# A two-block model on one core: router and last expert group in written order, the last group's first half in two column parts, MLP products of 512 and 256 columns

## The chip, the core and the metric

The kernel runs on one core of a Trainium2 chip, as one launch. The metric is device time in microseconds (us), the median of several executions. TensorE (PE) multiplies, VectorE (DVE), ScalarE (ACT) and GpSimd (POOL) work on SBUF and PSUM, and one DMA queue, issued by SyncE (SP), brings the weights from HBM. All dense data is float32. Durations are of one profiled execution.

## The reference

256 tokens of width 1024 go through two blocks of one layer each. The first block ends with a mixture of experts, the second with a gated MLP:

```python
def hier_moe(xn, w_group, b_group, w_er, b_er, w_e_in, w_e_out):
    g_logits = (xt @ w_group) + b_group
    g_sel = jnp.argmax(g_logits, axis=-1)                      # top-1 of 4 groups
    e_logits = ((xt @ w_er) + b_er).reshape(T, N_GROUPS, EXPERTS_PER_GROUP)
    e_in_group = jnp.take_along_axis(e_logits, g_sel[:, None, None], axis=1)[:, 0]
    top_v, top_i = lax.top_k(e_in_group, TOP_K_INNER)          # top-2 of its 8 experts
    gates = g_prob * jax.nn.softmax(top_v, axis=-1)
    ...
    hdn = lax.ragged_dot(xs, w_e_in, group_sizes)              # 1024 -> 2 x 256
    act = jax.nn.silu(gate_h) * up_h
    ys = lax.ragged_dot(act, w_e_out, group_sizes)             # 256 -> 1024
    ys = ys * gates...
    return jnp.zeros_like(xt).at[tok_sorted].add(ys)

# first block:  h = h + merged @ w_out;  h = h + hier_moe(rms_norm(h, norm2_g), ...);  rms_norm(h, norm_f_g)
# second block: h = rmsnorm(x, ln1); z = h @ w_in  (q, k, v of three attentions, three gates)
#               x = x + merged @ w_o
#               u = causal_dwconv(rmsnorm(x, ln2) @ w_up, conv_w, conv_b)   # 1024 -> 2 x 2816, 3 taps
#               a, b = split(u);  x = x + (silu(a) * b) @ w_down;  rmsnorm(x, ln_f)
```

## The kernel before

Tokens are held as two tiles of 128 (`t` = 0, 1). **Dense products** are made of three products each, to keep float32 precision: weights and activations are split into a high and a low part (`wh`, `wl`; `xx[:, 0]`, `xx[:, 1]`), and high by high, high by low and low by high are added in PSUM. `split` makes the two parts of a weight unit of 1024 columns: ACT copies the high part (L158), VectorE subtracts to get the low part (L159). Three buffers `w0` to `w2` hold split units. `mat_a` (L183 to L185) has the activations as the stationary operand and 512 columns of weights moving; `mat_b` (L190 to L192) has the weights stationary and the 256 tokens moving.

**Weights** come through `Ring`, a list of all loads in the order of their use on one SP queue (L81). A load is issued as soon as it is the next of the list and a slot of its size is free; `done(i)` gives a slot back. Dense units are 512 KB (tile `a`), expert units 1 MB (two of the `a` slots, or slots `r`, `rw`, `rc`). `rw` are the three buffers `w0` to `w2`, lent to the ring while the experts run.

**The router** (L678 to L790): the last dense product of the first block is added to `h` (L694, 512 columns at a time), `h` is transposed (L678), multiplied by the router's weights (L686, tile `prt`), scaled by the rms, and a chain of small VectorE operations picks group and experts of each token (`lgt` L718 to `cm` L730). A product with a triangular matrix gives each token its rank (L734), and from the ranks VectorE makes a selection matrix `sT` of 128 slots (L787, L788), one for each token tile. The gather multiplies `h` by `sT` (L796), `xg` is its result.

**The experts** run in eight groups of four, 32 slots for each. A group takes four pairs of units for the products in (L950), the gated unit, and two pairs of units for the products out (L962), one for each half (512 columns) of the output. The half's rows are multiplied by the gates and split (`yh` L853, `yl` L854), and the scatter (L861) adds them back to token order in `acc`, in PSUM, where `h` stands already. In the list of loads, two dense units of the second block stand ahead of the last two expert units. After the last group `acc` is copied to `h` (L913, L915), `h` is transposed (L922) and split (`uu`, L925, L926), and the second block's first dense product starts on it (`psa`, four units). The V product (L183 to L185 on `uu`) follows, then the rms statistics and their row (`prb`, L1093).

**The MLP** runs over 11 blocks `j` of 2 x 256 columns. `up(j)` is four units of eight 128-column blocks, `mat_b` each, into two PSUM banks; `gated(j)` scales (L1331), does the convolution (L1335 to L1337), silu and product, and splits the result (`ah`, `al`); `down(j)` multiplies by two units of `w_down` (L1362 to L1365, 512 columns). The order on TensorE is `up(j)`, `down(j - 1)`, `up(j + 1)`.

Inside `tc.manual_schedule(engines=...)` the listed engines keep the written order; elsewhere a scheduler orders instructions. PSUM has eight banks, four under the tag `mm` and four under `sm`.

Of the kernel before, what the change touches and what calls it, by code (L numbers as in the profile page):

```python
# [20 lines left out]
P = 128  # L21
# [80 lines left out]
def _build(ctx, tc, nc, a, out):  # L102
# [193 lines left out]
    def keep_warm(n):  # L296

        junk = sm([P, P], name="junk")
        for _ in range(n):
            nc.tensor.matmul(junk, warm, warm, start=True, stop=True)  # L300
# [374 lines left out]
    def h_turned(c, t):  # L675
        pt = sm([P, 4, P])
        for j in range(4):
            nc.tensor.transpose(pt[:, j, :], h[:, t, (4 * c + j) * P:(4 * c + j + 1) * P], ident)  # L678
        hT = m2.tile([P, 4, P], F32, name="hT", tag="hT", bufs=2)
        nc.vector.tensor_copy(hT[:, 0:2, :], pt[:, 0:2, :])  # L680
        nc.scalar.activation(hT[:, 2:4, :], pt[:, 2:4, :], AF.Copy)
        return hT

    def router(c, t, hT):
        for j in range(4):
            nc.tensor.matmul(prt[:, t, :], hT[:, j, :], wr[:, 4 * c + j, :], start=(c == 0 and t == 0 and j == 0),  # L686
                             stop=(c == 1 and j == 3), skip_group_check=True)
# [29 lines left out]
    def route(t):  # L717
        nc.vector.scalar_tensor_tensor(lgt[:, t, 0:36], prt[:, t, :], r2[:, t:t + 1], row("br"), op0=OP.mult, op1=OP.add)  # L718
        nc.vector.max(out=gm[:, t, :], in_=lgt[:, t, 32:40])
        nc.vector.max_index(out=gi[:, t, :], in_max=gm[:, t, :], in_values=lgt[:, t, 32:40])  # L720

        nc.vector.tensor_tensor(ohg[:, t], iota[:, 0:4], gi[:, t, 0:1].to_broadcast([P, 4]), op=OP.not_equal)
        nc.vector.scalar_tensor_tensor(em[:, t], ohg[:, t, :, None].to_broadcast([P, 4, 8]), -BIG,
                                       lgt[:, t, 0:32].rearrange("p (g e) -> p g e", e=8), op0=OP.mult, op1=OP.add)
# [13 lines left out]
    with tc.manual_schedule(engines={mybir.EngineType.PE}):  # L738
# [3 lines left out]
        for t in range(NT):  # L742
            add_to_h(0, t)
# [6 lines left out]
        for t in range(NT):  # L750
            for u in (2, 3):
                mat_a(mTh, mTl, pss, ww[u - 2], [(kk, t) for kk in range(2)], 2 * u, KD, 0, 512, 512)
                if (t, u) == (0, 2):
                    for t2 in range(NT):
                        router(0, t2, hTs[t2])
# [783 lines left out]
```

## Time and profile before

| | |
|---|---|
| median of 3 runs | 883.31 us (882.45 to 883.67) |
| profiled execution | 884.57 us, of which 882.84 are the span from first to last instruction |
| TensorE | busy 834.0 us (94%), mean granted clock 0.988 |
| VectorE | busy 528.7 us (60%) |
| ACT | busy 396.6 us (45%) |
| DMA | 217.79 MB, mean 247 GB/s |

Busy time of TensorE is a time in which at least one product was in flight; it says nothing of how fast the columns went through. Shares are means over stages that differ, so the rows further down are read by stage.

### The profile page before, as it was taken

To read this page: it belongs to the slowest core of one execution; us is meant where nothing else is said; L and a number is where in the kernel's file an instruction comes from. 1 tells how busy PE (TensorE), PEld (TensorE's weight loads), DVE (VectorE), ACT (ScalarE), POOL (GpSimd) and SP (SyncE) were. 2 spreads that over 40 slices of the span, in tenths; PEclk is the share of its full clock that TensorE was granted. 3 is DMA by queue.
4 is the path that set the end of the run, shared out by engine and by line. 5 is a ranking of instruction groups with operands and counts; after the bars stand their busy time and mean duration, and the time that the engine had idled before them with its cause. 6 is when DMAs were issued, how large, how long until landed. Compare 5 with 4: busy or idle time off the path is not lost.

```text
span 882.8 us, 13378 instructions
## 1 busy us (share of the span) xinstructions
PE 834.0 (94%) x5143; PEld 652.4 (74%) x5143; DVE 528.7 (60%) x1055; ACT 396.6 (45%) x621; POOL 34.4 (4%) x44
## 2 busy tenths in 40 slices
PE   7999999999999999778886999999999999999996
PEld 6878789988887544254331888778887999999995
DVE  7887866574565322123112867664496787767876
ACT  6444665554343011101111664575545556555554
POOL 3000101000000000000000100000030000000001
PEclk9999999999999999979999999999999999999999
DMA  8654536879968899999999573336555465555511
GB/s 329 271 167 165 179 130 235 316 248 326 331 267 322 336 422 422 419 418 420 420 421 407 180 234 127 107 120 198 195 166 190 162 192 190 180 188 182 176 62 48
DMA packets 48559, 217.79 MB, mean 247 GB/s; under 512 B 5616, under 2 KB 7296, under 8 KB 36200
## 3 DMA queue, kind: packets, MB, share of 16 engines
q1 hardware_dynamic: 47608, 215.00, 65.6%
q0 software_dynamic: 592, 1.84, 0.7%
q8 instruction: 42, 0.69, 0.3%
q14 instruction: 29, 0.24, 0.1%
q10 hardware_dynamic: 288, 0.03, 0.0%
HBM read 215.77 MB, written 1.07 MB: 246 GB/s over the span
## 4 chain that ended last, share of the span: by engine, by line
PE 49%; issue 26%; DMA 18%; DVE 3%; ACT 2%; POOL 1%; POOLq 0%; SPq 0%; DVEq 0%
PE mm L183 10%; PE mm L185 10%; PE mm L184 10%; DMA r<-in_u_exp 6%; DMA rw<-in_u_exp 5%; DMA a<-in_u_exp 5%; PE sm L950 2%; PE mm L191 2%; PE mm L190 2%; PE mm L192 2%; DVE ww L159 1%; PE sm L796 1%; ACT ww L158 1%; PE sm L1129 1%; PE po L1159 1%
## 5 line engine op out<-in xcount | busy, mean ns | idle before, releaser
L159 DVE TENSOR_TENSOR ww<-a,ww 128x1024 fp32r<-128x1024 f32 (+2 forms) x212 | 256.7, 1212 | 125.1 <-ACT ww L158 116.2
L158 ACT ACTIVATE ww<-a 128x1024 fp32r<-128x1024 f32 (+2 forms) x212 | 220.5, 1042 | 225.9 <-PE mm L185 115.7
L190 PE MATMUL sm<-zz,ww 128*128 128x256 f32 x352 | 99.8, 284 | 0.0
L191 PE MATMUL sm<-zz,ww 128*128 128x256 f32 x352 | 99.7, 283 | 0.0
L192 PE MATMUL sm<-zz,ww 128*128 128x256 f32 x352 | 99.6, 283 | 0.0
L184 PE MATMUL mm<-ww,xx 128*128 128x512 f32 x208 | 82.1, 395 | 3.5 <-DVE ww L159 3.5
L183 PE MATMUL mm<-ww,xx 128*128 128x512 f32 x208 | 82.4, 399 | 0.5 <-ACT ww L158 0.5
L185 PE MATMUL mm<-ww,xx 128*128 128x512 f32 x208 | 81.8, 393 | 0.0
L191 PEld LDWEIGHTS sm<-zz,ww 128*128 128x128 f32 x352 | 67.5, 192 | 0.4
L190 PEld LDWEIGHTS sm<-zz,ww 128*128 128x128 f32 x352 | 67.4, 192 | 0.4
L192 PEld LDWEIGHTS sm<-zz,ww 128*128 128x128 f32 x352 | 67.5, 192 | 0.0
L183 PE MATMUL mm<-ww,uu 128*128 128x512 f32 (+1 forms) x128 | 49.7, 388 | 0.0
L185 PE MATMUL mm<-ww,uu 128*128 128x512 f32 (+1 forms) x128 | 48.8, 381 | 0.0
L184 PE MATMUL mm<-ww,uu 128*128 128x512 f32 (+1 forms) x128 | 48.7, 380 | 0.0
L184 PEld LDWEIGHTS mm<-ww,xx 128*128 128x128 f32 x208 | 39.1, 188 | 12.3 <-DVE ww L159 4.7
L183 PEld LDWEIGHTS mm<-ww,xx 128*128 128x128 f32 x208 | 39.1, 188 | 8.5 <-ACT ww L158 0.7
L185 PEld LDWEIGHTS mm<-ww,xx 128*128 128x128 f32 x208 | 39.1, 188 | 7.9 <-issue 0.3
L950 PE MATMUL sm<-r,xg 128*32 128x512 f32 x304 | 42.4, 613 | 2.5 <-DMA r<-in_u_exp 2.5
L796 PEld LDWEIGHTS sm<-sT,h 128*128 128x128 f32 x256 | 31.9, 205 | 14.1 <-issue 12.9
L796 PE MATMUL sm<-sT,h 128*128 128x128 f32 x256 | 33.7, 293 | 7.3 <-DVE sT L788 7.2
L853 ACT ACTIVATE yh<-sm,sc 128x512 fp32r<-128x512 f32 x16 | 11.0, 687 | 56.9 <-PE sm L962 44.2
L841 ACT ACTIVATE G<-sm 128x256 fp32r<-128x256 f32 x8 | 3.1, 384 | 73.8 <-PE sm L837 73.8
(398 smaller groups left out, 1607.7 us busy)
## 6 DMA issues: line engine op xcount, KB each, us to landing
r<-in_u_exp SPq DMA_DIRECT2D x63, 1024.0 KB, 15.2
a<-in_u_mlp SPq DMA_DIRECT2D x66, 512.0 KB, 4.2
a<-in_u_in SPq DMA_DIRECT2D x59, 512.0 KB, 4.6
a<-in_u_exp SPq DMA_DIRECT2D x20, 1024.0 KB, 19.8
a<-in_u_c SPq DMA_DIRECT2D x40, 512.0 KB, 4.2
rw<-in_u_exp SPq DMA_DIRECT2D x9, 1024.0 KB, 20.0
a<-in_u_wa SPq DMA_DIRECT2D x8, 512.0 KB, 4.5
a<-in_u_wb SPq DMA_DIRECT2D x8, 512.0 KB, 5.8
```

The source lines that it names most:

```text
L158: nc.scalar.activation(wh[:, c:c + step], wt[:, c:c + step], AF.Copy)
L159: nc.vector.tensor_tensor(wl[:, c:c + step], wt[:, c:c + step], wh[:, c:c + step].bitcast(F32), op=OP.subtract)
L183: nc.tensor.matmul(pss[t], lh, rh, start=(k == 0), stop=False)
L184: nc.tensor.matmul(pss[t], lh, rl, start=False, stop=False)
L185: nc.tensor.matmul(pss[t], ll, rh, start=False, stop=(k == kt - 1))
L190: nc.tensor.matmul(ps, wh[:, c:c + P], xx[:, 0, k, :], start=(k == 0 and first), stop=False, skip_group_check=True)
L191: nc.tensor.matmul(ps, wh[:, c:c + P], xx[:, 1, k, :], start=False, stop=False, skip_group_check=True)
L192: nc.tensor.matmul(ps, wl[:, c:c + P], xx[:, 0, k, :], start=False, stop=(k == kt - 1), skip_group_check=True)
L796: nc.tensor.matmul(px[:, k2, :], h[:, t, (k + k2) * P:(k + k2 + 1) * P], sT[:, t, :], start=(t == 0), stop=(t == 1))
L853: nc.scalar.activation(yh, py, AF.Copy, scale=gs)
L950: nc.tensor.matmul(ph[32 * j:32 * j + 32, :], xg[:, k, 32 * j:32 * j + 32], us[j // 2][0][:, (2 * (j % 2) + kk) * 512:(2 * (j % 2) + kk + ...
L1129: nc.tensor.matmul(pl, qv[:, qt * P:(qt + 1) * P], kv[:, :nk], start=True, stop=extra is None)
```

## The change

It has three parts, which don't depend on each other.

**A. The router in written order.** TensorE, and from the last products of the second half on also VectorE and ACT, keep the written order. Both units' products of the first token tile come first, then those of the second tile; the first tile is added to `h`, transposed and put through its first selection steps meanwhile. The second tile's addition to `h` comes in two halves of 256 columns. The 13 steps of the two selection chains are dealt out in turn (`steps`), and the gather is split by token tile (`gather_part`). The three `w` buffers go to the ring one by one, each after its last use (`give`), instead of together.

**B. The last group.** Group 7 gets 24, 24, 24 and 18 small bf16 products on a junk bank behind its four pairs of products in, and 10 more at its end (`keep_warm`). The products out of the first half are made in two parts of 256 columns, and evacuated, scattered and summed by parts. Transposes and the first dense unit of the second block come before the products of the last half. Splits are made by 512 columns at fixed places, and the statistics' squares move ahead of units 2 and 3.

**C. The MLP's up-products.** For the first nine of eleven `j`, `wh` is multiplied by the high and low parts of `zz` together in one product of 512 columns, and `wl` by the high part in one of 256. The two halves of a bank must then be added: ACT copies one out of PSUM, VectorE adds the other (L1510), and `gated` works on the sum in SBUF. Four banks are used instead of two.

The core of the diff:

```diff
-    def add_to_h(c, t):
-        hv = h[:, t, c * 512:(c + 1) * 512]
-        nc.vector.tensor_tensor(hv, pss[t], hv, op=OP.add)
-        junk = sm([P, 512], name="junk")
-        nc.scalar.activation(junk, hv, AF.Square, accum_out=ss2[:, t, c:c + 1])
+    def add_to_h(c, t, c0=0, n=512):
+        hv = h[:, t, c * 512 + c0:c * 512 + c0 + n]
+        nc.vector.tensor_tensor(hv, pss[t][:, c0:c0 + n], hv, op=OP.add)
...
+        def give(x):
+            ring.add_slots(big.tile([P, 2, UNIT], F32, name="rw", tag=f"w{old_w[x]}", bufs=1), 1, 2, moe1 - 10)
+        give(0)
+        mat_a(mTh, mTl, pss, ww[0], [(kk, 0) for kk in range(2)], 4, KD, 0, 512, 512)
+        for t in range(NT):
+            router(0, t)
+        mat_a(mTh, mTl, pss, ww[1], [(kk, 0) for kk in range(2)], 6, KD, 0, 512, 512)
+    with tc.manual_schedule(engines={mybir.EngineType.PE, mybir.EngineType.DVE, mybir.EngineType.Activation}):
+        add_to_h(1, 0)
+        squares(1, 0)
+        mat_a(mTh, mTl, pss, ww[0], [(kk, 1) for kk in range(2)], 4, KD, 0, 512, 512)
+        give(1)
...
+        nc.vector.tensor_copy(hT[0], pt)
+        rms_of(1, 0)
+        mat_a(mTh, mTl, pss, ww[1], [(kk, 1) for kk in range(2)], 6, KD, 0, 512, 512)
         ring_blk(12, 2, moe1 - 14)
...
+        give(2)
+        r0, r1 = route(0), route(1)
+        for i in range(2):
+            add_to_h(1, 1, 256 * i, 256)
+        router(1, 0)
...
+        router(1, 1)
+        steps(r0, 2)
+        rms_of(1, 1)
+        steps(r0, 2)
...
+        for _ in range(5):
+            steps(r1, 1)
+            steps(r0, 1)
+        ranked(0, 0, oneb, code, first=True)
+        ranked(0, 0, upper, cm[:, 0, :], last=True)
...
+        for i in range(2):
+            gather_part(px[i], sT, 2 * i, 2, 0)
+        steps(r1, 4)
...
+            gather_part(px[i], sT, 2 * i, 2, 1)
+            gathered(px[i], xg, 2 * i, 2)
...
-    def products_in(q):
+    def products_in(q, junk):
...
+            if junk is not None:
+                keep_warm((24, 24, 24, 18)[u], junk)
...
+        for i, (w, _) in enumerate(us):
+            for c in range(2):
+                for kk in range(2):
+                    for j in (2 * i, 2 * i + 1):
+                        o = (2 * (j % 2) + kk) * 512 + 256 * c
+                        nc.tensor.matmul(py[c][32 * j:32 * j + 32, :], at[:, kk, 32 * j:32 * j + 32], w[:, o:o + 256],
...
+        rows_part(py[0], 0, 256)
+        scatter_part(0, 0, 256)
+        wh0(0)
+        sums_part(0, 0, 256)
+        rows_part(py[1], 256, 256)
+        wh0(512)
+        pts = turn_k((0, 1), sm)
...
+        unit_by_parts(psa, uu, 0, w0, 0)
+        pts = turn_k((2, 3), sm)
...
+        unit_by_parts(psa, uu, 0, w0, 1)
...
+        py = mm([P, 512])
+        for kk in range(2):
+            for j in range(4):
...
+        rows_part(py, 0, 512)
+        unit_by_parts(psa, uu, 1, w1, 0)
...
+        scatter_part(1, 0, 512)
...
+        unit_by_parts(psa, uu, 1, w1, 1, (0, 1))
...
+        pts = turn_k((4, 5, 6, 7), mm)
+        unit_by_parts(psa, uu, 1, w1, 1, (2, 3))
...
     def up(j):
-        pu = [sm([P, 2, S]) for _ in range(2)]
+        wide = j < NJ - 2
+        pu = [sm([P, 2, S]) for _ in range(4 if wide else 2)]
...
+                    if wide:
+                        nc.tensor.matmul(pu[b], wh[:, c:c + P], zz[:, :, k, :], start=(k == 0), stop=False, skip_group_check=True)
+                        nc.tensor.matmul(pu[b][:, 0, :], wl[:, c:c + P], zz[:, 0, k, :], start=False, stop=(k == KD - 1), skip_group_check=True)
+                    else:
+                        mat_b(pu[b // 2][:, b % 2, :], zz, wh, wl, c, k, KD, b % 2 == 0)
+        if not wide:
+            return pu
+        xs = [e1.tile([P, 2, S], F32, name=f"cx{i}", tag=f"cx{i}", bufs=2) for i in range(2)]
+        for b in range(4):
+            xv = xs[b // 2][:, b % 2, :]
+            nc.scalar.activation(xv, pu[b][:, 1, :], AF.Copy)
+            nc.vector.tensor_tensor(xv, pu[b][:, 0, :], xv, op=OP.add)
+        return xs
```

Where instructions stand. On TensorE, from the last dense products to the first expert products of group 0, before (L678 turns `h`, L686 the router's product, L734 the ranks, L796 the gather, L950 the expert product):

```order
L184 MATMUL mm<-ww,mT 128x512
L185 MATMUL mm<-ww,mT 128x512
L678 MATMUL sm<-ident,h 128x128 x8
L686 MATMUL prt<-wr,hT 128x36 x8
...
L734 MATMUL prk<-cm,upper 128x32
L782 LDWEIGHTS oneb
L782 MATMUL prk<-cm,oneb 128x32
L796 MATMUL sm<-sT,h 128x128 x8
L950 MATMUL sm<-r,xg 32x512 x8
```

and of the change (L684 turns, L688 the router's product, L750 the ranks, L758 the gather in parts, L995 the expert product):

```order
L684 MATMUL sm<-ident,h 128x128 x4
L183 MATMUL mm<-ww,mT 128x512
...
L688 MATMUL prt<-wr,xg 128x36 x4
L684 MATMUL sm<-ident,h 128x128 x2
L684 MATMUL mm<-ident,h 128x128 x2
L688 MATMUL prt<-wr,xg 128x36 x4
L754 MATMUL acc<-h,ident 128x512
...
L758 MATMUL px<-sT,h 128x128 x8
L995 MATMUL sm<-r,xg 32x512 x8
```

The first tile's transposes now stand ahead of the last dense products, and its router product ahead of the second tile's transposes. The eight gather products (four for each token tile) are one row in both; of the change the four of the first tile stand first.

On TensorE at the end of group 7, before (L962 the products out, L861 the scatter, L922 turns `h`, L190 to L192 the dense units of the second block):

```order
L861 MATMUL acc<-yh,G 128x512
L861 MATMUL acc<-yl,G 128x512
L861 MATMUL acc<-yh,G 128x512
L861 MATMUL acc<-yl,G 128x512
L962 MATMUL sm<-r,at 32x512 x8
L922 MATMUL sm<-ident,h 128x128 x8
L190 MATMUL mm<-uu,ww 128x256
```

and of the change (L1134 the products out of the first half, L1180 those of the last half, L1104 the scatter, L1090 turns `h`, L1081 the dense units):

```order
L1134 MATMUL sm<-r,at 32x256 x8
L1104 MATMUL acc<-yh,G 128x256 x2
L1104 MATMUL acc<-yl,G 128x256 x2
L1090 MATMUL sm<-ident,h 128x128 x4
L1104 MATMUL acc<-yh,G 128x256 x2
L1104 MATMUL acc<-yl,G 128x256 x2
L1081 MATMUL psa<-uu,ww 128x256 x12
L1090 MATMUL sm<-ident,h 128x128 x4
L1081 MATMUL psa<-uu,ww 128x256 x12
L1180 MATMUL mm<-r,at 32x512 x8
L1081 MATMUL psa<-uu,ww 128x256 x12
L1104 MATMUL acc<-yh,G 128x512 x2
```

Eight transposes and a whole dense unit (24 products) have moved ahead of the products out of the last half.

On VectorE in one period of the MLP, before (L1331 scales, L1336 and L1337 are the convolution, L159 splits, L1340 multiplies by silu, L233 makes `al`):

```order
L1331 TENSOR_TENSOR cx_10019<-sm,rb_8220 128x512
L1331 TENSOR_TENSOR cx_10020<-sm,rb_8220 128x512
L159 TENSOR_TENSOR ww<-a,ww 128x1024
L1336 SCALAR_TENSOR_TENSOR cy_10017<-cx_10019,cwb,cy_10017 128x255 x2
...
L159 TENSOR_TENSOR ww<-a,ww 128x1024
L1340 TENSOR_TENSOR sa<-sa,cy_10018 128x512
```

and of the change (L1510 adds the two halves of a bank, L1517 scales, L1522 and L1523 are the convolution, L1526 multiplies by silu):

```order
L1510 TENSOR_TENSOR cx_9604<-sm,cx_9604 128x256 x2
L1510 TENSOR_TENSOR cx_9605<-sm,cx_9605 128x256 x2
L1517 TENSOR_TENSOR cx_9604<-cx_9604,rb_8349 128x512
L1517 TENSOR_TENSOR cx_9605<-cx_9605,rb_8349 128x512
L159 TENSOR_TENSOR ww<-a,ww 128x1024
L1522 SCALAR_TENSOR_TENSOR cy_9646<-cx_9604,cwb,cy_9646 128x255 x2
...
L159 TENSOR_TENSOR ww<-a,ww 128x1024
L1526 TENSOR_TENSOR sa<-sa,cy_9646 128x512
```

Four additions have come in ahead of the scaling; the rest keeps its place.

## Rows read from the trace of the kernel before

**Rows 1.** Windows: busy time and count of each engine, clock, DMA share, GB/s.

```profile
core 0: us, PE busy (x) PEld busy (x) DVE busy (x) ACT busy (x) POOL busy (x), PEclk, DMA share, GB/s
288.00:292.00 4.00, 4.00 (x26) 2.46 (x30) 1.46 (x7) 0.00 (x0) 0.00 (x0) 0.63 0.86 360
320.00:480.00 160.00, 130.76 (x956) 61.56 (x959) 35.07 (x85) 17.68 (x31) 0.00 (x0) 0.97 1.01 419
480.00:484.00 4.00, 4.00 (x18) 1.22 (x16) 0.60 (x3) 0.00 (x0) 0.43 (x1) 0.57 1.04 409
760.00:800.00 40.00, 40.00 (x274) 37.14 (x273) 30.89 (x45) 22.98 (x31) 0.00 (x0) 1.00 0.56 185
```

**Rows 2.** The chain that ended last, 270 to 520 us: start, us, what.

```profile
340.17 19.82 DMA rw<-in_u_exp
...
479.90 4.49 DMA a<-in_u_c
```

**Rows 3.** Timeline of the router: start, us, engine, operation, [idle before, released by].

```profile
279.84 0.81 SPq L81 DMA_DIRECT2D r<-in_u_exp  x2
279.84 0.69 DVE L694 TENSOR_TENSOR h<-mm,h 128x512 f32<-128x512 f32 x1 [1.04 <-PE mm L185]
280.45 0.41 DVE L680 COPY hT<-sm 128x256 f32<-128x256 f32 x1
...
281.98 0.38 ACT L681 ACTIVATE hT<-sm 128x256 f32<-128x256 f32 x1 [0.36 <-DVE hT L680]
...
283.24 0.42 DVE L718 SCALAR_TENSOR_TENSOR lgt<-prt,r,rows 128x36 f32<-128x36 f32 x2 [0.87 <-PE prt L686]
...
287.37 2.82 PE L796 MATMUL sm<-sT,h 128*128 128x128 f32 x16 [0.49 <-DVE sT L788]
287.46 0.35 DVE L788 SCALAR_TENSOR_TENSOR sT<-rows,cg,e 128x128 f32<-128x128 f32 x1
...
290.12 3.04 PE L950 MATMUL sm<-r,xg 128*32 128x512 f32 x16
...
293.21 0.95 SPq L81 DMA_DIRECT2D r<-in_u_exp  x2
```

**Rows 4.** Windows of 1 us where the DMA queue is empty, columns as in rows 1.

```profile
291.00:292.00 1.00, 1.00 (x12) 0.34 (x8) 0.00 (x0) 0.00 (x0) 0.00 (x0) 0.50 0.40 156
292.00:293.00 1.00, 1.00 (x12) 0.03 (x4) 0.00 (x0) 0.00 (x0) 0.00 (x0) 0.78 0.00 0
```

**Rows 5.** Timeline from group 7 to the V products, TensorE alone.

```profile
452.75 1.92 PE L950 MATMUL sm<-r,xg 128*32 128x512 f32 x16
...
473.23 1.03 PE L962 MATMUL sm<-r,at 128*32 128x512 f32 x4
...
479.88 3.39 PE L962 MATMUL sm<-r,at 128*32 128x512 f32 x12 [1.34 <-DMA r<-in_u_exp]
...
487.84 0.50 PE L861 MATMUL acc<-yl,G 128*128 128x512 f32 x1 [0.87 <-DVE yl L854]
...
492.25 1.04 PE L922 MATMUL sm<-ident,h 128*128 128x128 f32 x8
...
500.91 0.40 PE L183 MATMUL mm<-ww,uu 128*128 128x512 f32 x1
...
503.66 0.59 PE L1093 MATMUL sm<-dg,gfd 128*128 128x256 f32 x2
```

**Rows 6.** Timeline of one period of the MLP, its turning points.

```profile
744.61 0.39 PE L1362 MATMUL acc<-ww,ah 128*128 128x512 f32 x1
...
750.19 0.28 PE L190 MATMUL sm<-zz,ww 128*128 128x256 f32 x1
750.20 1.22 DVE L159 TENSOR_TENSOR ww<-a,ww 128x1024 fp32r<-128x1024 f32 x1
...
761.70 0.39 PE L1362 MATMUL acc<-ww,ah 128*128 128x512 f32 x1
```

More of the change, by code (lines that the diff above doesn't have):

```diff
@@ new lines, in steps, with ranked, sums_from_h, gather_part @@
+    def steps(q, n):
+        for _ in range(n):
+            q.popleft()()
+    def ranked(t, i, by, cm_, first=False, last=False):
+        nc.tensor.matmul(prk[t][:, i, :], by, cm_, start=first, stop=last, skip_group_check=True)
+    def sums_from_h(hf, t):
+        nc.tensor.matmul(acc[t][hf], ident, h[:, t, hf * 512:(hf + 1) * 512], start=True, stop=False, skip_group_check=True)
+    def gather_part(px, sT, k, m, t):
+        for k2 in range(m):
+            nc.tensor.matmul(px[:, k2, :], h[:, t, (k + k2) * P:(k + k2 + 1) * P], sT[:, t, :],
+                             start=(t == 0 and k2 == 0), stop=(t == 1), skip_group_check=True)
@@ new lines, in _build @@
+        ranked(0, 0, upper, cm[:, 0, :], last=True)
+        sums_from_h(0, 1)
+        for _ in range(4):
+            steps(r1, 1)
+            steps(r0, 1)
+        ranked(1, 0, oneb, code, first=True)
+        ranked(1, 0, oneb, cm[:, 0, :])
+        ranked(1, 0, upper, cm[:, 1, :], last=True)
+        ranked(1, 1, oneb, cm[:, 0, :])
+        ranked(1, 1, oneb, cm[:, 1, :], last=True)
+        px = [sm([P, 2, P], name="px") for _ in range(2)]
+        for i in range(2):
+            gather_part(px[i], sT, 2 * i, 2, 0)
@@ L1041, in _build, with halves @@
-    for u in (2, 3):
-        unit_b(psa, uu, u, weights(1024))
+        junk = sm([P, P], name="junk")
+        at, G, gs, _ = group(7, junk)
+        keep_warm(10, junk)
+    def halves(wt):
+        w = turn[0] % 3
+        turn[0] += 1
+        ww = big.tile([P, 2, UNIT], F32R, name="ww", tag=f"w{w}", bufs=1)
+        wh, wl = ww[:, 0, :], ww[:, 1, :]
+        return (wh, wl), lambda c: nc.scalar.activation(wh[:, c:c + 512], wt[:, c:c + 512], AF.Copy), \
+            lambda c: nc.vector.tensor_tensor(wl[:, c:c + 512], wt[:, c:c + 512], wh[:, c:c + 512].bitcast(F32), op=OP.subtract)
@@ new lines, in unit_by_parts, with turn_k @@
+    def unit_by_parts(pss, xx, u, ww, kk, bs=range(4), kt=KD):
+        wh, wl = ww
+        k = 2 * u + kk
+        for i, (w, x) in enumerate(((wh, 0), (wl, 0), (wh, 1))):
+            for b in bs:
+                c = kk * 512 + b * P
+                nc.tensor.matmul(pss[b // 2][:, b % 2, :], w[:, c:c + P], xx[:, x, k, :], start=(k == 0 and b % 2 == 0 and i == 0),
+                                 stop=(k == kt - 1 and i == 2), skip_group_check=True)
+    def turn_k(ks, pool):
+        pts = []
+        for k in ks:
+            pt = pool([P, S])
+            for t in range(NT):
+                nc.tensor.transpose(pt[:, t * P:(t + 1) * P], h[:, t, k * P:(k + 1) * P], ident)
+            pts.append(pt)
+        return pts
```

339 lines of the change are left out of this document (191 added, 148 removed).

## The prediction

> **What bounds the kernel now.** I read the windows first, to see which engine is full in which stage. Three kinds of stage matter here. From 320 to 480 us, the expert stage, the DMA share is 1.01 at 419 GB/s, while TensorE is busy for 130.76 of 160 us and VectorE for 35.07 [rows 1]: the stage ends when its bytes have come, and nothing that an engine does inside it can shorten it. The chain of waits says the same: its pieces there are DMA alone, the first listed at 340.17, the last landing on unit `a` at 479.90 [rows 2]. In the MLP, 760 to 800 us, TensorE is busy all 40 us, VectorE 30.89, the DMA share is 0.56 [rows 1]: there a TensorE product saved is time saved. Between them, 480 to 484, TensorE counts as busy but its granted clock is 0.57, and between 288 and 292 it is 0.63 [rows 1].
>
> Then I read the timeline at the two borders of the DMA stage. At the front border the queue runs dry: of 291 to 292 the DMA share is 0.40, of 292 to 293 it is 0.00 [rows 4], because the next unit is issued at 293.21, when the first expert products are done with theirs [rows 3]. So whatever brings those products forward moves the entire DMA stage forward. At the rear border everything that follows the last landing, 479.88, until the next stage that TensorE fills (the V products, 500.91), is on the path: 21.03 us [rows 5].
>
> **Part A, the router.** Before: the logits of both token tiles go through VectorE as one interleaved chain from 283.24 to 287.81 (287.46 + 0.35), the gather starts at 287.37, takes 2.82 us, and the first expert products run from 290.12 to 293.16 (3.04 us) [rows 3]. After: the first tile's first steps are over before the second tile's logits come, its gather stands before the second tile's selection, and side steps (three of some 0.15 us) have left the chain. The second tile's logits come no earlier: its last dense product now has four transposes ahead of it, and its addition to `h` is cut in two halves (0.41 for 256 columns out of PSUM instead of 0.69 [rows 3]), which about cancel. I put the second selection matrix at 287.2, 0.6 earlier: the chain's 4.57 us without 0.6 for steps done early and 0.45 of side steps, with 0.4 given back where a step waits for the rank product on TensorE. Behind it only half of the gather remains, so that the products start at about 288.4 instead of 290.12, with the same length at the same clock: **1.7 us**. Lower bound 0.2 (the chains in written order wait for each other, and only the gather's overlap is left), upper bound 2.8 (TensorE's pause is shorter, the clock stays at its upper level, and the 16 rows take 1.92 as in [rows 5] instead of 3.04). The slots handed to the queue earlier change only where the queue idles, not whether: it has as many slots as before and is dry in both cases before the products release one. All of the saving comes out at 479.88, since nothing between waits for anything but bytes.
>
> **Part B, the last group.** Work after the last landing, before: 12 of the 16 rows of the second half's products (an expert product of 512 columns is two rows of the trace), 8 transposes, one and a half of 24-product dense units, a scatter of 4, units 2 and 3. Much stands still: 12 rows take 3.39 us where 16 take 1.92 at the upper clock, and the scatter waits 0.87 for VectorE's `yl` [rows 5]. After: the first dense unit, the first half's scatter and the first transposes stand before the landing. Can they be done by then? The first half's products ended at 474.26 (473.23 + 1.03 [rows 5]); behind them come the evacuations of 256 columns on ACT and VectorE (0.38 and 0.41 [rows 3]), scatter, sums, transposes, splits, and 24 products of 0.12: I add this up to 480.7, so 0.8 us of unit 0 lies behind the landing. Then the second half's products (16 rows, 1.9), unit 1 (24 x 0.120 = 2.9), the scatter (4 x 0.229 = 0.9, the spacing of 512 columns in [rows 5], 12 in 2.75 us), 8 transposes (1.0), units 2 and 3 (48 x 0.120 = 5.8): 13.3, and 0.3 for waits on the two other engines, 13.6 against 21.03. That is 7.4. The row scale's product, formerly 12 products into the V stage (500.91 to 503.66 [rows 5]), comes after 24 now but with a stage that starts 7 us earlier; I allow 0.4 for waiting there, an estimate. Net **7.0 us**, from 4.5 (ACT's and VectorE's written order makes one 1.2 us split late at two places) to 8.5. The junk products lie in waits: two 1 MB units come in 5.0 us at 419 GB/s [rows 1], their products take 1.92 [rows 5]. I cost them at nothing; if TensorE were still in junk when a pair lands, at most some 0.8 us of a pair shows, and the last pair of group 7 alone counts.
>
> **Part C, the MLP.** One period is 17.09 us (744.61 to 761.70): 24 products of 512 columns in 5.58 us, 0.2325 each, and 96 of 256 columns in 11.51, 0.120 each [rows 6]. Nine of the eleven up-products change from 96 x 256 columns to 32 x 512 and 32 x 256. At 0.2325 a wide one, this is 32 x 0.3525 = 11.28, 0.23 saved; at the V stage's 0.229, 11.17, 0.34 saved. Nine times: 2.1 to 3.1, middle 2.6.
>
> The Trainium skill, "TensorE: Matmul & The Clock Gate", section "Wait — 56ns, not 53.3ns?", speaks against this part: it puts one product at N columns over 2.4 GHz and a fixed 2.5 ns, by which two 256-column products would cost only 2.5 ns more than one of 512, and the 288 joined pairs 0.7 us in all, an estimate from that page. The trace does not agree: it has 7.5 to 11 ns for a pair, by the two spacings above.
>
> What C adds: per up-product four ACT copies (0.38 each by [rows 3]) and four VectorE additions (0.41 each), and all four small PSUM banks are in use instead of two. The last bank's addition ends about 1 us behind the up-product, and the next up-product comes 5.58 us of `down` later [rows 6], so the copies hide. VectorE's load rises from 30.89 of 40, 13.2 per period, by 1.65 to 14.9 of 16.85 [rows 1]. The tightest place is the split behind the convolutions, which ended at 751.42 (750.20 + 1.22); its first product is due behind one unit of the next up-product, at 753.2 (750.19 + 24 x 0.120 and the first wide one) [rows 6]. Of these 1.8 us the additions and the scaling behind them take 1.1 to 1.5, so that 0.3 to 0.7 us of room are left. Only between the first and second up-product no `down` stands, and there I allow 0.3 us (0 to 1.5). Net **2.3 us**, from 0 to 3.1.
>
> **Sum.** 1.7 + 7.0 + 2.3 = 11.0 us of the profiled execution's 884.57 (span 882.84, the rest around it unchanged): 873.6. That execution is 1.3 above the median of 883.31, so **872.3**.
>
> **Rivals.**
> - *A moves nothing* (the second tile's chain ends as late as before, or the slots' new order costs what the chain saves). For it: the chain is serial on VectorE, 4.57 us long. Against: half the gather leaves the path whatever it does. Time 874.0.
> - *C is set by columns alone*: a wide product costs what two narrow ones do, 2 x 0.120, since as many columns go through as before. For it: 7.5 ns are 3% of a product. Against: both spacings are of this kernel and this stage. C then gives nothing but its 0.3 us of waiting, time 874.9. By the rule of the Trainium skill's page named above it would be 0.7 better than that, 874.2, which tells the two apart no more than the measurement can.
> - *B gives half*: a split or evacuation in ACT's or VectorE's new written order stands behind one that waits for TensorE, as `yl` does now. For it: 480 to 492 holds some 30 operations on two engines that each wait for the other. Gain 3.5, time 875.8.
> - *Slower, VectorE becomes the bound of the MLP.* Place: that split behind the convolutions, with TensorE waiting for it after the first unit of each later up-product. Price: it decides from a stall of 11.0 / 9 = 1.2 us in each of nine periods. For it: only 0.3 to 0.7 us of room, and a late split delays the next one's buffer. Against: a stall gives VectorE, idle for 2 us of the new period, time to catch up, so that it would have to run 1.5 to 1.9 us later than I count. With a stall of 1.5 us the time would be 885.
>
> **Chances.** My forecast 0.46, A nothing 0.14, C by columns 0.15, B half 0.16, slower 0.05, several of these together 0.04. A difference under 0.2% (1.8 us) can't be told from none. Faster 0.92, same 0.03, slower 0.05. Range: all upper bounds together (2.8 + 8.5 + 3.1 = 14.4) reach 868.9; B half with A nothing reach 877.5, with C by columns as well 880.1. I take 868.9 to 879.0.
>
> **What the profile of the changed kernel would show.** A: the issue that stands at 293.21 comes at about 291.5, the last landing at about 478.2. If the issue moves and the landing doesn't, the DMA stage had another bound. B: from the last landing to the first V product 13 to 14 us instead of 21.03, the clock at its upper level in the products behind the landing. C: a period of about 16.8 us with TensorE busy throughout and no wait in front of the first wide product of a later up-product. The prediction is wrong if the time from landing to V products stays above 17 us, if TensorE idles in the MLP, or if the period is above 17.

## The result, and the profile after

The changed kernel takes 871.29 us (median of 4 executions, 871.04 to 871.55), the kernel before 883.49 in the same series (882.45 to 884.27): ratio 0.9863 with an interval of 0.9846 to 0.988, 12.2 us or 1.4% faster. Forecast were 872.3 and 11.0 us. The profiled execution took 871.04 us, 13.5 less than that of before, with a span of 869.3. These 13.5 us lie here (us from the start of the span, and lengths):

| stretch | before | after | gain |
|---|---|---|---|
| router's first transposes to the issue that ends the DMA queue's gap | 271.47 to 293.21 | 271.47 to 290.27 | 2.9 |
| that issue to the first V product | to 500.91 | to 489.22 | 8.75 |
| V products to the end | 381.9 | 380.1 | 1.8 |

Timeline of the router after, the rows that answer to [rows 3] (start, us, engine, operation, idle before):

```profile
280.30 0.76 DVE L695 TENSOR_TENSOR h<-mm,h 128x256 f32<-128x256 f32 x2 [0.63 <-PE mm L185]
...
281.77 0.24 DVE L727 SCALAR_TENSOR_TENSOR lgt<-prt,r,rows 128x36 f32<-128x36 f32 x1
...
282.94 0.25 DVE L727 SCALAR_TENSOR_TENSOR lgt<-prt,r,rows 128x36 f32<-128x36 f32 x1 [0.25 <-POOL r L706]
...
285.87 2.38 PE L758 MATMUL px<-sT,h 128*128 128x128 f32 x16
...
286.68 0.35 DVE L743 SCALAR_TENSOR_TENSOR sT<-rows,cg,e 128x128 f32<-128x128 f32 x1
...
287.84 0.87 DVE L762 TENSOR_TENSOR xg<-px,pp 128x256 f32<-128x256 f32 x2 [0.57 <-PE px L758]
...
288.32 1.93 PE L995 MATMUL sm<-r,xg 128*32 128x512 f32 x16
...
290.27 1.14 SPq L81 DMA_DIRECT2D r<-in_u_exp  x2
```

The first tile's logits (`lgt`) come at 281.77, the second's at 282.94 (283.24 before). The second selection matrix is done at 287.03, 0.78 earlier than 287.81; behind it half of the gather remains and the products start at 288.32, forecast 288.4. But they take 1.93 us, not 3.04: the windows say why (busy time and count of TensorE, its weight loads, VectorE, ACT, GpSimd, then granted clock, DMA share, GB/s), to be read beside [rows 1]:

```profile
288.00:292.00 4.00, 3.93 (x35) 2.30 (x33) 1.73 (x11) 1.34 (x6) 0.00 (x0) 1.00 0.77 272
320.00:480.00 160.00, 138.59 (x1102) 73.21 (x1095) 39.37 (x93) 22.68 (x43) 0.93 (x2) 0.97 1.01 419
480.00:484.00 4.00, 4.00 (x32) 3.67 (x31) 3.38 (x8) 2.77 (x7) 0.35 (x2) 1.00 0.97 363
```

The granted clock is 1.00 at both borders of the expert stage, where it was 0.63 and 0.57. The stage itself is unchanged: DMA share 1.01, 419 GB/s.

Timeline of TensorE behind group 7, and of ACT where it says so, the answer to [rows 5]:

```profile
475.11 1.68 PE L1081 MATMUL psa<-uu,ww 128*128 128x256 f32 x12
...
476.71 1.92 PE L1180 MATMUL mm<-r,at 128*32 128x512 f32 x16
477.36 1.15 ACT L1071 ACTIVATE ww<-a 128x512 fp32r<-128x512 f32 x2 [0.46 <-DMA a<-in_u_c]
...
478.56 1.69 PE L1081 MATMUL psa<-uu,ww 128*128 128x256 f32 x12
...
480.09 0.63 PE L1104 MATMUL acc<-yh,G 128*128 128x512 f32 x2
...
481.82 1.09 PE L1090 MATMUL mm<-ident,h 128*128 128x128 f32 x8
...
482.67 6.72 PE L1081 MATMUL psa<-uu,ww 128*128 128x256 f32 x54
...
489.22 0.40 PE L183 MATMUL mm<-ww,uu 128*128 128x512 f32 x1
```

L1180, the products of the last half, wait for nothing: TensorE comes from the first dense unit at 476.7, and all their bytes are there. The landing itself has no row. ACT waits until 477.36 for the next dense unit, 512 KB or 1.25 us of the queue at 419 GB/s, so the last expert unit landed at about 476.1, an estimate, 0.6 before TensorE was free. From there to the V products it is 13.1 us (21.03 before).

One period of the MLP after, TensorE, the answer to [rows 6]:

```profile
754.97 0.39 PE L1500 MATMUL sm<-zz,ww 128*128 128x512 f32 x1
...
766.26 0.39 PE L1548 MATMUL acc<-ww,ah 128*128 128x512 f32 x1
...
771.84 0.40 PE L1500 MATMUL sm<-zz,ww 128*128 128x512 f32 x1
772.08 0.27 PE L1501 MATMUL sm<-zz,ww 128*128 128x256 f32 x1
772.19 0.40 PE L1500 MATMUL sm<-zz,ww 128*128 128x512 f32 x1
...
782.95 0.39 PE L1548 MATMUL acc<-ww,ah 128*128 128x512 f32 x1
```

Of the 16.69 us from 766.26 on, `down` takes the same 5.58 and the 32 pairs (one wide product and one narrow) take 11.11, 0.347 each where three narrow ones took 0.360. The up-product ahead of it, from 754.97, took 11.29, 0.353 a pair. Of the seven that follow the second, four take 11.10 or 11.11 and three 11.25 to 11.29. VectorE's split behind the convolutions and what stands ahead of it, for the question of its room:

```profile
765.88 1.42 DVE L1510 TENSOR_TENSOR cx<-sm,cx 128x256 f32<-128x256 f32 x4
767.22 1.28 DVE L1517 TENSOR_TENSOR cx<-cx,rb 128x512 f32<-128x512 f32 x2
...
772.71 1.22 DVE L159 TENSOR_TENSOR ww<-a,ww 128x1024 fp32r<-128x1024 f32 x1
```

### The profile page after: what moved, and what is told of

Same layout as the page of the kernel before. It is cut to its first block, busy times and chain, and to the rows that moved or that the text cites. A ratio compares the mean times of both kernels' runs of the same rounds, so it can differ in the third digit from the quotient of the medians.

```text
span 869.3 us, 13138 instructions
## 1 busy us (share of the span) xinstructions
PE 830.9 (96%) x4975; PEld 642.8 (74%) x4975; DVE 540.6 (62%) x1100; ACT 408.5 (47%) x663; POOL 33.5 (4%) x44
## 4 chain that ended last, share of the span: by engine, by line
PE 51%; issue 26%; DMA 17%; DVE 3%; ACT 2%; POOL 1%; POOLq 0%; SPq 0%; DVEq 0%
PE mm L183 11%; PE mm L185 11%; PE mm L184 11%; DMA r<-in_u_exp 9%; DMA rw<-in_u_exp 2%; DMA a<-in_u_exp 2%; DMA rc<-in_u_exp 2%; PE mm L190 2%; PE sm L995 2%; PE mm L191 2%; PE mm L192 2%; PE psa L1081 1%; PE sm L887 1%; DVE ww L159 1%; PE sm L1301 1%
## 5 line engine op out<-in xcount | busy, mean ns | idle before, releaser
L159 DVE TENSOR_TENSOR ww<-a,ww 128x1024 fp32r<-128x1024 f32 (+2 forms) x206 | 249.5, 1213 | 109.0 <-ACT ww L158 104.0
L158 ACT ACTIVATE ww<-a 128x1024 fp32r<-128x1024 f32 (+2 forms) x206 | 214.3, 1041 | 203.4 <-PE mm L185 114.2
L1500 PE MATMUL sm<-zz,ww 128*128 128x512 f32 x288 | 101.5, 397 | 0.4 <-DVE zz L1462 0.4
L1501 PE MATMUL sm<-zz,ww 128*128 128x256 f32 x288 | 80.1, 280 | 0.0
L1500 PEld LDWEIGHTS sm<-zz,ww 128*128 128x128 f32 x288 | 53.9, 188 | 13.1 <-DVE zz L1462 0.7
L1501 PEld LDWEIGHTS sm<-zz,ww 128*128 128x128 f32 x288 | 54.2, 188 | 0.5
L995 PE MATMUL sm<-r,xg 128*32 128x512 f32 x328 | 43.8, 596 | 2.0 <-DMA r<-in_u_exp 1.9
L887 PEld LDWEIGHTS sm<-sT,h 128*128 128x128 f32 x240 | 29.6, 204 | 12.6 <-issue 12.6
L887 PE MATMUL sm<-sT,h 128*128 128x128 f32 x240 | 30.9, 290 | 6.7 <-DVE sT L879 6.7
L1549 PE MATMUL acc<-ww,ah 128*128 128x512 f32 (+1 forms) x90 | 35.0, 389 | 0.0
L1551 PE MATMUL acc<-ww,al 128*128 128x512 f32 (+1 forms) x90 | 35.0, 389 | 0.0
L1548 PE MATMUL acc<-ww,ah 128*128 128x512 f32 (+1 forms) x90 | 35.0, 389 | 0.0
```

The costliest lines, as they stand in the source:

```text
L158: nc.scalar.activation(wh[:, c:c + step], wt[:, c:c + step], AF.Copy)
L159: nc.vector.tensor_tensor(wl[:, c:c + step], wt[:, c:c + step], wh[:, c:c + step].bitcast(F32), op=OP.subtract)
L887: nc.tensor.matmul(px[:, k2, :], h[:, t, (k + k2) * P:(k + k2 + 1) * P], sT[:, t, :], start=(t == 0), stop=(t == 1))
L995: nc.tensor.matmul(ph[32 * j:32 * j + 32, :], xg[:, k, 32 * j:32 * j + 32], us[j // 2][0][:, (2 * (j % 2) + kk) * 512:(2 * (j % 2) + kk + ...
L1500: nc.tensor.matmul(pu[b], wh[:, c:c + P], zz[:, :, k, :], start=(k == 0), stop=False, skip_group_check=True)
L1501: nc.tensor.matmul(pu[b][:, 0, :], wl[:, c:c + P], zz[:, 0, k, :], start=False, stop=(k == KD - 1), skip_group_check=True)
```

## The experiments

The kernels of one series ran on one chip, against the kernel before; the series ran on different chips, so that kernels of two series are compared by their ratios to before. A distance given below runs from the router's first eight transposes, which are alike in all these kernels; that start itself lies at 271.1 to 271.5 or at 272.8 to 273.3 in the profiled executions, whatever the kernel.

**The parts alone.** Each is the diff's part on the kernel before, nothing else:

```
 a_only:  router in written order, give(), gather_part(); tail and up() as before
 b_only:  group(7, junk), two column parts, unit 0 first; router and up() as before
 c_only:  up(j) wide for j < 9; router and tail as before
```

> The kernel before with part A alone (router in written order, buffers handed over one by one). Theory 1, from the two traces: A is worth 3.5 us, 2.9 of it because the first expert products are done at 290.2 instead of 293.16 (TensorE's clock stays at its upper level there), the rest because the DMA queue's gap behind it is shorter; time 3.5 under before, ratio 0.996. Theory 2, the prediction's size: 1.7 us, ratio 0.998. In both the stage behind the last landing stays 21 us long.

> The kernel before with part B alone (last group in written order, junk products, the first dense unit ahead of the last half's products). Theory 1, from the two traces: 8.2 us, the V products begin 12.8 us behind the last landing; ratio 0.9907. Theory 2, the prediction's size: 7.0 us, 14 us behind the landing, ratio 0.992. The last landing stays near 479.8.

> The kernel before with part C alone (one product of 512 and one of 256 columns in nine up-products). Theory 1: a period of 16.7 to 16.85 us instead of 17.09, less a wait of 0.4 at the start: 2.2 to 2.6 us, ratio 0.9972. Theory 2, columns alone set the time of a product: a period of 17.1, nothing gained, 0.4 lost. If the parts don't touch each other, the three gains add up to that of the whole change, 12.2 us.

Measured: A 0.9967 (0.9953 to 0.9981), B 0.9922 (0.9897 to 0.9947), C 0.9975 (0.9959 to 0.9991). In us of 883 that is A 2.9 (1.7 to 4.2), B 6.9 (4.7 to 9.1), C 2.2 (0.8 to 3.6). For B the prediction's size (theory 2) is nearer than 8.2, for C theory 1 holds; for A 2.9 lies between the two, nearer 3.5, and its interval reaches both. The three gains add up to 0.0136, and the whole change has 0.0137. So nothing shows that the parts touch each other; with these intervals an effect of 2 to 3 us between them could hide. What is most worth reading is the profile of C alone, whose router and tail are those of before. Its windows at the two borders and, of B alone, two windows of the router (columns as above):

```profile
288.00:292.00 4.00, 3.41 (x29) 2.35 (x32) 2.80 (x16) 0.00 (x0) 0.00 (x0) 1.00 1.01 426
478.00:482.00 4.00, 2.76 (x20) 1.25 (x20) 0.71 (x3) 0.23 (x1) 0.54 (x1) 1.00 1.03 409
```

```profile
284.00:288.00 4.00, 2.87 (x9) 0.84 (x7) 2.85 (x22) 2.01 (x6) 0.00 (x0) 0.71 1.02 428
288.00:292.00 4.00, 3.97 (x32) 2.29 (x32) 2.02 (x12) 0.00 (x0) 0.00 (x0) 1.00 0.79 328
```

Timeline of C alone, TensorE's rows at the two places, with VectorE's second selection matrix between:

```profile
288.74 2.32 PE L796 MATMUL sm<-sT,h 128*128 128x128 f32 x16 [0.49 <-DVE sT L788]
288.83 0.35 DVE L788 SCALAR_TENSOR_TENSOR sT<-rows,cg,e 128x128 f32<-128x128 f32 x1
290.99 1.92 PE L950 MATMUL sm<-r,xg 128*32 128x512 f32 x16
292.94 1.60 SPq L81 DMA_DIRECT2D r<-in_u_exp  x2
...
479.24 1.91 PE L962 MATMUL sm<-r,at 128*32 128x512 f32 x12 [1.39 <-DMA r<-in_u_exp]
...
498.63 0.40 PE L183 MATMUL mm<-ww,uu 128*128 128x512 f32 x1
```

In this execution of the same code the clock did not fall. From the router's transposes (272.84) to the issue it is 20.10 us, not 21.74, and from the last landing to the V products 19.39, not 21.03; A alone, with the same tail, has 19.39 too. So 1.64 and 1.64 us of what the profile of before shows at these borders are the clock of that execution, and not the code. At the front, 0.50 of them lie between the second selection matrix and the first expert products (2.31 us before, 1.81 here) and 1.14 between the start of these products and the issue (3.09 and 1.95). B alone, with the same router, has a third distance, 21.02, and its clock fell at another place: it is 0.71 from 284 to 288 and back at 1.00 from 288 on, where before has 0.63. The ten executions with A's router that were profiled have 18.80 or 18.81, every one.

**The changed kernel again, and its spread.** No edit.

> The changed kernel again, as the reference of this series. Theory 1, formed from the profile of C alone: the kernel before loses up to 3.6 us to TensorE's lower clock at the two borders of the expert stage, in some executions and not in others, and the change takes that away; so the changed kernel's executions lie closer together (under 1.5 us) than those of before (879 to 886), and the granted clock of before goes with its time. Theory 2: the spread is of the chip and both have it.

Measured: 870.69 (870.12 to 871.92), ratio 0.9875 (0.9858 to 0.9892); before 880.7 to 885.48 in the same series. Theory 1 asked for a spread under 1.5 us: it is 1.8, against 4.8 of before, but over 4 executions against 9, and more executions spread wider by themselves. In 23 executions of before in the first series the three of the lowest mean clock (0.986, 0.987) took 886, the two of the highest (0.992) 879.3 and 881.2. In the other series the order is looser: of this one, two executions at 0.993 took 882.5 and 882.9.

**Junk products in the kernel before**, to hold the clock up without moving anything:

```diff
+        junk = sm([P, P], name="junk")
+        keep_warm(10, junk)
         ranks(0)
...
+        keep_warm(6, junk)
         ranks(1)
...
+        keep_warm(12, junk)
...
+        at, G, gs, _ = group(7, junk)
+        keep_warm(10, junk)
         py = products_out(at)
+        keep_warm(12, junk)
...
         scatter(0, G, ys, True)
+        keep_warm(30, junk)
```

> The kernel before with junk products (bf16, 128 columns) in TensorE's waits at both borders of the expert stage: 10, 6 and 12 in the router, 24, 24, 24, 18 and 10 in group 7, 12 and 30 between the products out; nothing else is moved. Theory 1, the lower clock at the borders costs the kernel before 0 to 3.6 us, differently in each execution, and the change's gain holds this share: the executions come together near the fastest of before, the median 1.5 to 3 us under before's (ratio 0.997 to 0.998), the 12 rows behind the landing take 1.9 us. Theory 2, the spread has another cause: same median, same spread.

Measured: ratio 0.999 (0.9976 to 1.0004), 879.99 to 883.71 against 880.66 to 885.4. The clock is at 1.00 in all windows from 280 to 296 and from 470 to 490, and the 12 rows behind the landing take 1.91. But the distance to the issue is 20.81, 0.7 more than with the clock up and no junk: the junk stands in the router's way. Theory 1 is right in what the clock does; its 1.5 to 3 us are not there. The median gains 0.7 us, and the interval reaches from 0.4 slower to 2.1 faster, so that no gain is shown. If the 0.7 that the junk costs are given back, about 1.5 of the 12.2 us would be the clock; that is an estimate, and these runs leave room for 0.4 to 2.8.

**The buffers handed over together**, as before:

```diff
-        give(0)
...
-        give(1)
...
-        give(2)
...
         sums_from_h(0, 1)
+        for x in range(3):
+            give(x)
```

> The changed kernel with the three weight buffers handed to the ring together, behind the ranks' products, where the kernel before has it, instead of one by one. Theory 1, the queue runs dry before the next release in any case, and earlier hand-over moves only where it idles: same time within 0.3 us, the gap just before 280 longer and that at 290 shorter. Theory 2, the three 1 MB loads keep the queue busy until the release at 290: 0.5 to 2 us slower than the change.

Measured: 870.61, ratio 0.9877 (0.986 to 0.9894), to the changed kernel's 0.9875: no difference. The issue comes 18.81 us behind the start again, and the V products 217.4 (the change: 217.3 and 217.75). Windows of 2 us of this kernel (columns as above), where the queue now idles for all of 280 to 282 and hardly at 292:

```profile
280.00:282.00 2.00, 2.00 (x14) 1.74 (x13) 1.14 (x4) 0.00 (x0) 0.57 (x1) 1.00 0.01 4
292.00:294.00 2.00, 2.00 (x22) 1.58 (x25) 0.41 (x1) 0.00 (x0) 0.00 (x0) 1.00 0.96 336
```

Theory 1 holds: earlier hand-over only moves the gap.

**The gather behind the second selection.** The gather of the first tile was written behind `steps(r1, 4)`:

```diff
-        for i in range(2):
-            gather_part(px[i], sT, 2 * i, 2, 0)
         steps(r1, 4)
+        for i in range(2):
+            gather_part(px[i], sT, 2 * i, 2, 0)
```

> The changed kernel with the gather of the first token tile moved behind the selection of the second. Theory 1, the split gather is the main part of A: the first expert products start 0.7 to 1.2 us later (from router transposes to the next issue 19.6 to 20 us instead of 18.8), time 0.7 to 1.2 above the change; if the clock falls, 2.5. Theory 2, the chain on VectorE carries A: under 0.3.

This failed as an experiment: the two lines go to different engines, each engine's list of instructions stays what it was, and the kernel that ran is the changed kernel. It is a repeat, 871.52 (0.9877) beside 870.69 (0.9875), and shows what the medians of one program differ by, 0.8 us. Its question stays without an experiment. What the split gather is worth was read from the rows instead: with the clock up in both, the second selection matrix is done 16.34 us behind the start in the profile of C alone (288.83 + 0.35) and 15.56 after; from there to the first expert products it is 1.81 and 1.29. So the chain gives 0.78 and the gather 0.52, together the 1.30 between 20.10 and 18.80.

**The first dense unit behind the last half's products:**

```diff
-        unit_by_parts(psa, uu, 0, w0, 0)
...
-        unit_by_parts(psa, uu, 0, w0, 1)
...
         rows_part(py, 0, 512)
+        unit_by_parts(psa, uu, 0, w0, 0)
+        unit_by_parts(psa, uu, 0, w0, 1)
         unit_by_parts(psa, uu, 1, w1, 0)
```

> The changed kernel with the first dense unit of the second block (24 products) behind the last half's products instead of ahead of them. Theory 1, everything behind the last landing is on the path: 24 x 0.12 = 2.9 us less what stood behind the landing anyway (0.3 to 0.8), 2.1 to 2.6 us slower, if the clock falls in the wait up to 4. Theory 2, the stage is set by ACT's and VectorE's splits of the later units, not by TensorE: under 1 us slower.

Measured: 873.77 against 870.69, 3.1 slower (ratio 0.9911, 0.9897 to 0.9925). In the profiles it is 1.2 to 2.1: 219.27 to the V products, where the six profiles with the change's last group and junk have 217.15 to 218.07. TensorE now waits for the last unit again:

```profile
475.20 1.91 PE L1178 MATMUL mm<-r,at 128*32 128x512 f32 x12 [0.91 <-DMA r<-in_u_exp]
477.04 4.57 PE L1081 MATMUL psa<-uu,ww 128*128 128x256 f32 x36
...
490.52 0.40 PE L183 MATMUL mm<-ww,uu 128*128 128x512 f32 x1
```

The landing is at 475.2, the V products 15.3 us later, 2.2 more than the change's 13.1, as theory 1 has it (2.1 to 2.6): what moves behind the landing is on the path.

**No junk in group 7:**

```diff
-        at, G, gs, _ = group(7, junk)
-        keep_warm(10, junk)
+        at, G, gs, _ = group(7)
```

> The changed kernel without the junk products of group 7. Theory 1: they keep the clock up, and without them the last group's products behind the landing run at about half the clock: about 1.5 to 2 us slower than the change (3.39 us for 12 rows stood there before). Theory 2: the work that now stands ahead of the landing (a dense unit, scatter, transposes) keeps the clock up by itself, and the junk is worth nothing: within 0.5 us of the change. Theory 3: the junk delays a pair of products and its absence gains up to 0.8 us.

Measured: ratio 0.9898 (0.9877 to 0.9918), whose interval overlaps that of the change, and 219.24 to the V products, 1.2 to 2.1 later than in those six profiles. It looked like theory 1, but the clock behind the landing was 1.00; of the windows read from 460 on it was below that, at 0.70, only at 460 to 464, where TensorE waits for bytes anyway. VectorE's timeline, with three rows of TensorE's, showed another cause:

```profile
476.96 1.92 PE L1178 MATMUL mm<-r,at 128*32 128x512 f32 x16
...
479.04 0.27 DVE L1238 MEMSET cband<- 128x256 f32 x1 [1.08 <-PE mm L1178]
479.30 0.23 DVE L1372 MEMSET lw<- 128x200 f32 x1
479.53 0.27 DVE L1377 MEMSET tri<- 128x256 f32 x1
479.71 1.42 DVE L1070 TENSOR_TENSOR ww<-a,ww 128x512 fp32r<-128x512 f32 x2
481.06 0.74 DVE L1107 SCALAR_TENSOR_TENSOR yl<-mm,sc,yh 128x512 fp32r<-128x512 f32 x1
...
481.85 0.74 PE L1102 MATMUL acc<-yl,G 128*128 128x512 f32 x2 [0.88 <-DVE yl L1107]
...
490.58 0.40 PE L183 MATMUL mm<-ww,uu 128*128 128x512 f32 x1
```

Three fills of later tiles, which the scheduler may place between the written instructions, had come to stand ahead of a split and of `yl`. The first waits 1.08 us for the last half's products, and TensorE 0.88 for `yl`. In the changed kernel they stand behind the split. The test puts them on GpSimd, whose rows in these traces name SBUF tiles alone, as these three are:

```diff
-    nc.vector.memset(cband, 0.0)
+    nc.gpsimd.memset(cband, 0.0)
...
-    nc.vector.memset(lw, 0.0)
+    nc.gpsimd.memset(lw, 0.0)
...
-    nc.vector.memset(tri, 1.0)
+    nc.gpsimd.memset(tri, 1.0)
```

> The changed kernel without the junk products of group 7 and with three fills (cband, lw, tri), which the scheduler put into VectorE's queue there, on GpSimd instead. Theory 1, from the profile without junk: what that kernel lost behind the landing (V products 219.24 us behind the router's first transposes instead of 217.3 to 217.8) is a wait of the fills for the last half's products, with a split and yl queued behind them, and not the clock, which was at its upper level; so the distance returns to 217.0 to 217.6 and the ratio to before to 0.9865 to 0.988. Theory 2, the junk itself is worth 1 us or more, by the clock or otherwise: the distance stays at 219, the ratio at 0.99.

Measured: 871.22, ratio 0.9876 (0.9854 to 0.9897), as the changed kernel; 218.3 to the V products, over the expected 217.0 to 217.6. TensorE's rows divide it:

```profile
476.97 1.92 PE L1178 MATMUL mm<-r,at 128*32 128x512 f32 x16
...
489.43 0.40 PE L183 MATMUL mm<-ww,uu 128*128 128x512 f32 x1
```

From the start of the last half's products to the V products it is 13.62 us without junk, 12.46 with the fills moved, and 12.45 to 12.51 in those six profiles: the fills cost 1.1 us, and moving them gives all of it back. The rest lies ahead of these products, which start 205.83 us behind the router's transposes here and 205.62 without junk, 204.69 to 205.62 in the six profiles. So the junk products are worth nothing that these runs can show.

**More work for VectorE in the MLP.** Two maxima of a tile with itself in each period:

```diff
             nc.vector.tensor_tensor(xv, pu[b][:, 0, :], xv, op=OP.add)
+        for i in range(2):
+            nc.vector.tensor_tensor(xs[i], xs[i], xs[i], op=OP.max)
```

> The changed kernel with one more VectorE operation for each 512 columns of the summed up-products (a maximum with itself, two of 0.68 us in each of nine periods, right behind the additions), results unchanged. Theory 1, VectorE has 0.3 to 0.7 us of room there: of 1.36 us some 0.7 to 1 shows as a wait of TensorE, 6 to 9 us slower than the change. Theory 2, its 2 us of idle time in a period take all of it up: under 0.5 us slower. Theory 3, each operation costs its full time: 12 us slower.

Measured: 872.98, ratio 0.9882 (0.9862 to 0.9901), 0.6 above the changed kernel by the ratios, which the intervals don't tell from none, and 0.8 to 1.2 by the profiles (381.2 from the V products to the end, where seven profiles with the change's MLP have 380.0 to 380.4). Of 1.28 us in each of nine periods, 11.5, about a tenth shows in the profile, and TensorE's waits for a late split (L159) are 0.3 us in the whole MLP. None of the three theories holds; the second is nearest. It is no clean test, since the scheduler answered it. Two rows of TensorE's timeline:

```profile
759.87 1.08 PE L1500 MATMUL sm<-zz,ww 128*128 128x512 f32 x4
760.79 0.63 PE L1501 MATMUL sm<-zz,ww 128*128 128x256 f32 x4
```

Four products with the high weights in a row, and then the four with the low part that came late: the order on TensorE, free in the MLP, had been changed so that the wait is filled.

**A tenth wide up-product:**

```diff
-        wide = j < NJ - 2
+        wide = j < NJ - 1
```

(and the same bound in `gated`).

> The changed kernel with the tenth up-product in 512 and 256 columns as well. Theory 1: 0.23 to 0.35 us for one more, less a wait of the eleventh, which follows without a down-product between and needs two banks that are still to be added up: from 0.3 faster to 0.5 slower than the change. Theory 2, the wait is as long as the whole evacuation: 1 us slower.

Measured: 872.99, ratio 0.9891 (0.9871 to 0.991), whose interval overlaps that of the change; from the V products to the end 380.8, some 0.4 to 0.8 more. But the MLP is not slower: from the V products to the start of the last TensorE product it is 372.44 us here and 372.49 in the change. The tenth up-product saves 0.2, and the eleventh loses most of it, 11.61 us instead of 11.52 and a start 0.1 later. The 0.8 lie behind the last product (8.37 us to the end, 7.5 to 7.6 in all the other kernels), where the output is stored, and the tenth up-product has no part in that. So by the rows theory 1 holds, with nothing gained, and theory 2's wait is not there. No version was found that beats the change.

## Why the prediction was right, point by point

**The bound of the expert stage** held: 419 GB/s and a share of 1.01 in both, and in A alone what ends the gap at the front moved the end. The chain in [rows 2] was read too simply. The row at 479.90 is the transfer of the next dense unit, and the chain ahead of it has a TensorE product and an issue between transfers:

```profile
462.40 1.91 PE sm L950 x12
464.37 0.42 SPq L81
464.84 14.99 DMA r<-in_u_exp
```

Before 340.17 it runs mostly through TensorE. So "DMA alone" is too much for the chain; the DMA share of 1.01 is what carries the reading.

**A, forecast 1.7, with bounds of 0.2 and 2.8.** By the runs of A alone 2.9, by the two profiles 2.94 up to the issue. The chain gives 0.78 (forecast 0.6): the second tile's logits come 0.30 earlier, where the forecast had them no earlier, and the chain behind them is 0.48 shorter. From the second matrix to the products it is 1.29 instead of 2.31, 1.02 (forecast 1.1); but half of that is the clock, since C alone has 1.81 there, and the split gather itself is worth 0.52. What made A larger than the forecast is the step "with the same length at the same clock": the products took 1.93 in place of 3.04, the upper bound's case. That the clock would not fall was priced as a bound and not as the likely case, and the profile of before was taken for what the kernel always does; by C alone it is one of its cases. Another 0.7 us lie between issue and landing (A alone lands 2.0 us earlier than C alone by the distance, 204.4 against 206.4, for an issue 1.3 earlier); the runs don't say why, since the stage behind the issue varies by 1.7 us over the profiled executions.

**B, forecast 7.0.** By the runs of B alone 6.9. The working came close where it was made of TensorE rows: about 0.6 of unit 0 behind the landing (forecast 0.8), 13.1 us from landing to V products (13.6), no wait for the row scale's product beyond 0.3 (173.2 us from the V products to the MLP's first transposes before, 173.5 after). But 1.64 us of the 21.03 that it was taken from are the lower clock of that execution; against C alone, at the upper clock, the stretch shrank by 6.3 and not by 7.9. So at equal clock B is worth about 6, and its 7.0 holds part of the clock. The junk was costed at nothing, and it gave nothing that shows.

**C, forecast 2.3.** By the runs of C alone 2.2, by the profile 1.8 from the V products on, with those 0.3 included. In the seven up-products that follow the second, a pair saves 7 to 8 ns in three and 12.5 in four, 10.4 in the mean, inside the forecast's 7.5 to 11: 0.33 us each. The 0.3 allowed for the first two was needed, but for another wait. Nothing waits between them for banks; TensorE waits for the activations inside the first:

```profile
679.35 0.50 PE L1500 MATMUL sm<-zz,ww 128*128 128x512 f32 x1 [0.39 <-DVE zz L1462]
```

The two gain together nothing (the time from the first transposes to the first `down` is 36.4 after, 36.3 before).

**The rivals.** *A moves nothing*: it moved 2.9. *C set by columns alone*: fell with the pair's 0.347 to 0.353 against 0.360. By that rule of the Trainium skill, "TensorE: Matmul & The Clock Gate", section "Wait — 56ns, not 53.3ns?", a joined pair saves 2.5 ns; the trace does not agree, it has 7 to 12.5. *B gives half*: fell; yet the mechanism it named is real, and the kernel without junk shows it (`yl` behind a fill that waits for TensorE, 0.88 us). *VectorE as the bound of the MLP*: its split behind the convolutions ends at 773.93, its first product is due at about 774.85 (771.84 and eight pairs and one wide), so 0.9 us of room were left and not 0.3 to 0.7. In the run with more work for VectorE the 1.28 us exceeded that, and the scheduler's other order took up most of it. The price of this rival was added up wrong: nine stalls of 1.5 us on 872.3 give 885.8, not 885.

So 1.6 us of lower clock stand twice in the profile of before: the forecast counted those at the tail into B's gain, and of those at the front 0.5 into A's and 1.1 not. The median of before, 1.1 under its profiled execution, holds less of both. The mechanisms of the three parts are shown. At equal clock the rows give A 1.3 up to the issue and 0.7 behind it that stay unexplained, B about 6 and C 2.2, some 10 us; the rest of the 12.2 is clock and spread, which no run here divides. That 11.0 came so close to the median is in part luck.

## What to carry to other kernels

A stretch that is short of TensorE work, in front of a stage that is bound by bytes, is paid in full, and its price can differ from execution to execution with the clock; look at a second profile of the same code there before you take its durations for the kernel's. Work that needs none of the awaited bytes belongs ahead of the wait: 24 products moved there were worth 1.2 to 2.1 us by the profiles and 3.1 by the medians. Inside a written order, look for what the scheduler may still insert in the other engines' queues, since a fill that waits holds up what is queued behind it: three fills cost 1.1 us here.

## What was not expected of the hardware

The same router lost its upper clock at different places, or nowhere, in three profiled executions: in one the granted clock was 0.63 from 288 to 292, in another 0.71 from 284 to 288 and 1.00 behind that, in the third 1.00 throughout (a window's value is a mean of the two levels, 0.50 at 1.2 GHz and 1.00 at 2.4). The stretch took 21.74, 21.02 and 20.10 us. With other waits in it (A's router) it was 18.80 or 18.81 in ten of ten. What decides it in the kernel before stays open here.
